# A hybrid flow step on one NeuronCore: weight loads from the Fourier branch on issued by GpSimd in place of SyncE

## The chip, the core and the metric

The kernel runs on one NeuronCore of one Trainium2 chip. In the profile the core's engines are called PE (TensorE, matrix multiplication), PEld (its weight loads), DVE (VectorE), ACT (ScalarE), POOL (GpSimd) and SP (SyncE, which here only issues DMAs). DMAs are issued from three places, SP, ACT and POOL, each with a queue of its own; an engine works off its own instructions, DMA issues among them, in one fixed order, and an instruction that waits for a semaphore keeps everything behind it on the same engine waiting.

The metric is the device time of one execution in microseconds, as the median of several runs.

## What is computed

One layer of a backbone that mixes tokens in three parallel branches, for 2048 sample tokens and 128 prompt tokens of width 1024. Cut to what matters here, the reference is:

```python
proj = jnp.einsum('btd,de->bte', xn, w_in)
qkv, beta, dec, z_a, u_b, v_b, z_b, x_c, z_c, gates = jnp.split(proj, points, axis=-1)
...
o, s_f, s_b = delta_bidir(q, k, v, g, beta, s0_f, s0_b)       # branch A, chunks of 64 in a scan
o_b = chunk_sgu(u_b, v_b, sgu_norm_g, w_spatial, b_spatial) * jax.nn.silu(z_b)   # branch B
o_c = fourier_mix(x_c, grid) * jax.nn.silu(z_c)               # branch C, Fourier over tokens
...
br = jnp.stack([o_a, o_b, o_c], axis=2)
pb = jnp.einsum('btnw,nwd->btnd', br, w_branch)
gt = jax.nn.sigmoid(gates.reshape(B, T, N_BRANCH, D_MODEL))
merged = jnp.einsum('btnd,btnd->btd', gt, pb)
return jnp.einsum('btd,de->bte', merged, w_out), s_f, s_b
```

Everything is float32. The kernel reaches that accuracy with float16 matmuls: each operand is split into a scaled high part and the remainder, and a product takes three matmuls.

## The kernel before, in words

**The long row of matmuls.** The input projection is cut into blocks of 128 output columns: 60 blocks of w_in, 512 KB each, and with the last 24 of them (the merge gates) 24 blocks of w_branch, 256 KB each. They are used in one order, which `wlist` holds: 4 blocks of z_a, 12 of q, k and v, 4 of v_b, 8 of u_b and z_b in turn, then from number 28 on 8 of x_c and z_c in turn (the Fourier branch), and from number 36 on a gate block and a w_branch block in turn, branch B first, then C, then A. A block is multiplied with all 2176 tokens, in five token blocks (four of 512, one of 128), by `gemm_T` at line 250.

**How a block gets ready.** `read_w` (line 291 is its DMA's issue) loads a block into a staging tile of tag `wst`, of which there are two. `converting` then works in four steps: ACT squares the block to sum it (line 315), PE and DVE make a scale of the sum (lines 264 and 277 to 279), ACT writes the scaled high part (line 327), DVE the remainder (line 328). Only after line 328 is the staging tile free for the load after next. `weight_step`, called after each token block, takes one such step; `read_next` issues the next load two steps after a conversion has ended, and at most two blocks ahead. Two other users share the tag `wst`: `gate_rows` (line 1773) and the rows at the very end (lines 1907 and 1920); their loads are issued by SP.

**The second string of work.** Branch A is not done ahead of or after these matmuls but between them. A generator (`delta`) is advanced by `pace` a step at a time as the matmuls go on: first `prep` for the 17 token chunks, with `base_inverse` (POOL and DVE in turn, lines 1114 and 1115), then `scan` (34 steps: the chunks forwards, then backwards). A step of the scan loads from SP its chunk's arrays (ES at line 1171, N at 1175, sn at 1177, sk at 1268, skn at 1270, sv at 1272, sqk at 1322) and does short matmuls; POOL copies ES into T and R (lines 1188 and 1190) and scales skn (line 1295) and kn (line 1298). After the last gate block the products are merged (POOL adds into mrow, line 1739, and stores it) and multiplied with w_out.

**Who decides the order.** The program's text gives priorities. The order on each engine, SP's and POOL's queues included, is laid down when the program is built, by a planner that plays through a time line with a cost for every instruction (`TileContext(nc, schedule_with_timeline_sim=True)`). At run time that order is fixed; only semaphores decide when each instruction goes.

**Queues.** `load` (line 284) issues on SP; early in the program, while `turn_of` is set, it also fixes the order of the loads, and from about the third block on it is a plain `SY.dma_start`. POOL so far issues stores only: qkv, kv, nd, br, the merged rows, tw and pa. `G` is the wrapper around GpSimd; it passes `dma_start` on as it is.

Of the kernel before, what the change touches and what calls it, by code (L numbers as in the profile page):

```python
# [34 lines left out]
CQ = 545  # L35
FS = 4096.0
VS = 2048.0
ADA_D = (6, 7, 12, 13, 14, 15)
TBS = [(0, 512), (512, 512), (1024, 512), (1536, 512), (2048, 128)]

# [80 lines left out]
def _by_block(w, starts, width=P):  # L121


    w = np.asarray(w)
    return np.ascontiguousarray(np.stack([w[:, c0:c0 + width].reshape(-1, P, width).transpose(1, 0, 2).reshape(P, -1) for c0 in starts]))
# [17 lines left out]
def _ada_blocks(w):  # L143


    wide = _by_block(w[:, 0:2 * D], range(0, 2 * D, 2 * P), 2 * P).reshape(8, P, 2, D).transpose(0, 2, 1, 3).reshape(16, P, D)
    return np.ascontiguousarray(np.stack([w[:, b * P:(b + 1) * P].T if b in ADA_D else wide[b] for b in range(16)]))

# [46 lines left out]
def hybrid_flow_kernel(ctx: ExitStack, tc: tile.TileContext, x_prompt, x_sample, state_delta, c, c_ctx, w_ada,  # L195
# [4 lines left out]
    G, V, A, PE = [_InTurn(tc, e_) for e_ in (nc.gpsimd, nc.vector, nc.scalar, nc.tensor)]  # L200
# [9 lines left out]
    def sb(pl, shape, tag, dt=F32, bufs=None):  # L210
        kw = {} if bufs is None else {"bufs": bufs}
        return pl.tile(list(shape), dt, tag=tag, name=nm(tag), **kw)
# [69 lines left out]
    def load_w(src, nkt, cols=P, hi=None, lo=None, tag="w", bufs=5):  # L282
        return convert(read_w(src, nkt, cols, tag), nkt, cols, hi, lo, tag, bufs)
# [3 lines left out]
    def load(dst, src):  # L287


        if turn_of[0] is None:  # L290
            return SY.dma_start(dst, src)
        with tc.issue_after(turn_of[0].ins):
            turn_of[0] = SY.dma_start(dst, src)
        return turn_of[0]

    def read_w(src, nkt, cols=P, tag="w"):
        st = sb(wp, [P, nkt, cols], "wst" if cols == P else tag + "st", bufs=2 if cols == P else 1)
        load(st, src.rearrange("p (k c) -> p k c", c=cols))
        return st

    bsums = sb(cp, [P, 27], "bsums")
# [65 lines left out]
    wdone, wnext, wread, wlate, bwp, wsteps = [], [0], [], [0], [], []  # L367

    def read_next(p_=None):
        if p_ is not None:  # L370
            st = sb(p_, [P, D], "ab", bufs=7).rearrange("p (k c) -> p k c", k=KT)
            load(st, wlist[len(wread)][0].rearrange("p (k c) -> p k c", k=KT))
            wread.append(st)
        elif len(wread) < min(len(wdone) - len(wsteps) + 2, len(wlist)):
            src, nkt, tag, bufs = wlist[len(wread)][0:4]
            wread.append(read_w(src, nkt))
# [275 lines left out]
    load_xt(1)  # L652
    behind = load(cst[:, P:_CF], consts[:, P:_CF])
    bdst = read_w(w_bd, KT, 16, "d")
    turn_of[0] = None
    bound(1)
# [830 lines left out]
    vg = sb(bp, [P, 4], "vg", bufs=1)  # L1487
    V.tensor_scalar(vg, pc[:, 44:48], winv_, 1.0 / VS, ALU.mult, ALU.mult)
    vinv = sb(ep, [P, 4], "vinv", bufs=1)
# [17 lines left out]
    for t in range(NCH):  # L1507
# [12 lines left out]
        made = A.activation(v2[:, 1], vn, AF.Square, accum_out=ss)  # L1520
        V.tensor_scalar(ss, ss, 1.0 / WB / VS ** 2, EPS / VS ** 2, ALU.mult, ALU.add)
        G.tensor_tensor(ss, ss, mhalf, ALU.pow)
# [20 lines left out]
    for g in range(4):  # L1543
# [5 lines left out]
        for ti, (t0, tn) in enumerate(TBS):  # L1549
            st = vrow[:, t0:t0 + tn]  # L1550
# [638 lines left out]
```

## Time and profile before

| | |
|---|---|
| time, median of 3 runs | 2138.12 us (2137.19 to 2139.33) |
| the profiled execution, its time | 2138.49 us |
| its span in the trace | 2136.7 us |
| PE busy | 2081.9 us, 97% of the span |
| DVE, ACT, POOL busy | 62%, 50%, 40% |
| DMA by SP's queue | 290.58 MB, 42.3% of the DMA engines' time |
| DMA by POOL's queue | 65.89 MB, 8.2% |
| DMA by ACT's queue | 44.05 MB, 6.0% |

A page of the profile comes from one execution. "Busy" counts work, not waits, and not the issuing of DMAs. A row of the timeline reads: start, duration, engine and source line, operation, what is written and read, shapes, and in brackets how long the engine had been idle and who ended that. A row of the waits reads: who waited for whom, us in total, how often, the longest. In a row of the windows the engines' busy times are followed by the clock that PE was granted (1.00 is full speed), the share of the DMA engines and GB/s. A row of the issues reads: written and read, the queue, how often, size, median us from issue to landing.

### The profile page before, as it was taken

Reading aid. Unit: us, or ns where it says so; the run is one execution under the profiler, and the core shown is the slowest. Engines: PE = TensorE matmul, PEld = TensorE weight load, DVE = VectorE, ACT = ScalarE, POOL = GpSimd, SP = SyncE. Lnnn points to the kernel's source line nnn. Section 1 sums busy time; section 2 is a strip of 40 time slices with the busy share of each in tenths; the row PEclk is TensorE's granted clock in tenths of the full one; section 3 lists DMA queues with packets and bytes.
Section 4 is the critical chain, followed back from the end, with each engine's and each line's share of the span. In section 5 each row is a group of like instructions: output and inputs, shape, how many; then the busy total and the mean of one; then the engine's idle time right before and its main releaser. Section 6 shows DMA issues by size and latency. Waiting matters only on the chain.

```text
span 2136.7 us, 42553 instructions
## 1 busy us (share of the span) xinstructions
PE 2081.9 (97%) x16133; PEld 1196.5 (56%) x16133; DVE 1326.9 (62%) x2945; ACT 1059.7 (50%) x2456; POOL 844.5 (40%) x1089
## 2 busy tenths in 40 slices
PE   7999999999999999989999999999999999999998
PEld 4454444455555678778565556565655444444443
DVE  6656854379777786556755555866665554666245
ACT  5554744465665664445644445765653443453112
POOL 0321332225465554543321233355542234333464
PEclk9999999999999999999999999999999999999999
DMA  9525722177767744444655555767764644456862
GB/s 354 221 78 188 271 103 103 62 222 232 254 222 247 217 162 133 110 133 128 228 178 168 168 162 185 236 203 233 210 207 131 218 163 165 173 193 236 343 221 89
DMA packets 222286, 403.24 MB, mean 189 GB/s; under 512 B 39225, under 2 KB 109137, under 8 KB 219265
## 3 DMA queue, kind: packets, MB, share of 16 engines
q1 hardware_dynamic: 167040, 290.58, 42.3%
q0 software_dynamic: 15216, 65.89, 8.2%
q10 hardware_dynamic: 39824, 44.05, 6.0%
q8 instruction: 127, 2.08, 0.4%
q14 instruction: 79, 0.64, 0.1%
HBM read 258.19 MB, written 142.24 MB: 187 GB/s over the span
## 4 chain that ended last, share of the span: by engine, by line
PE 53%; DVE 7%; DMA 5%; POOL 4%; ACT 3%; issue 3%; SPq 0%; ACTq 0%; POOLq 0%; DVEq 0%
PE b L250 52%; POOL E L1115 1%; DMA tw<-tw 1%; DVE XB L1114 1%; POOL st L1466 1%; DMA sqk<-qk 1%; DMA ei<-XB 1%; ACT nd L1066 0%; DMA wst<-in_w_blk_dram 0%; DVE XB L1123 0%; PE b L1382 0%; POOL ss L1024 0%; DMA br<-st 0%; DMA skn<-kv 0%; DVE xh L182 0%
## 5 line engine op out<-in xcount | busy, mean ns | idle before, releaser
L250 PE MATMUL b<-xh,whi 128*128 128x512 f16 (+1 forms) x1920 | 651.0, 348 | 1.7 <-DVE sg L1456 1.6
L250 PE MATMUL b<-xl,whi 128*128 128x512 f16 (+1 forms) x1920 | 651.1, 348 | 0.0
L250 PE MATMUL b<-xh,wlo 128*128 128x512 f16 (+1 forms) x1920 | 650.2, 347 | 0.0
L250 PEld LDWEIGHTS <-whi 128*128 128x128 f16 x3856 | 352.5, 98 | 324.8 <-issue 6.1
L250 PEld LDWEIGHTS <-wlo 128*128 128x128 f16 x1928 | 188.8, 98 | 175.8 <-issue 1.8
L250 PE MATMUL b<-big,bhi 128*128 128x512 f16 (+1 forms) x960 | 250.2, 347 | 0.1
L250 PE MATMUL b<-big,blo 128*128 128x512 f16 (+1 forms) x480 | 163.1, 347 | 0.0
L1739 POOL TENSOR_TENSOR mrow<-mrow,sg 128x512 f32<-128x512 f32 (+1 forms) x80 | 95.3, 1193 | 127.7 <-DVE sg L1738 103.4
L953 POOL TENSOR_TENSOR cy<-cy,raw 128x545 f32<-128x545 f32 (+1 forms) x48 | 65.5, 1390 | 182.7 <-ACT raw L952 182.7
L250 PEld LDWEIGHTS <-xh 128*128 128x128 f16 x1496 | 117.0, 98 | 29.0 <-issue 1.5
L250 PEld LDWEIGHTS <-bhi 128*128 128x128 f16 x960 | 87.5, 98 | 76.7 <-issue 0.2
L1115 POOL TENSOR_TENSOR E<-E,XB 128x31 f32<-128x31 f32 (+15 forms) x155 | 94.6, 610 | 85.3 <-DVE XB L1114 68.6
L250 PEld LDWEIGHTS <-xl 128*128 128x128 f16 x1068 | 98.1, 98 | 45.9 <-DMA tw<-tw 2.4
L1729 ACT ACTIVATE sg<-b,winv 128x512 f32<-128x512 f32 (+1 forms) x120 | 74.0, 617 | 93.4 <-PE b L250 92.4
L1188 POOL COPY T<-ES 32x256 f16<-32x256 f16 x68 | 31.9, 470 | 177.0 <-DMA ES<-ei 144.6
L250 PE MATMUL b<-whi,xh 128*128 128x128 f16 x544 | 92.8, 219 | 0.0
L250 PE MATMUL b<-whi,xl 128*128 128x128 f16 x544 | 92.8, 219 | 0.0
L250 PE MATMUL b<-wlo,xh 128*128 128x128 f16 x544 | 92.8, 219 | 0.0
L328 DVE SCALAR_TENSOR_TENSOR wlo<-wst,wsc,whi 128x1024 f16<-128x1024 f32 x52 | 71.0, 1368 | 30.2 <-ACT whi L327 29.0
L1295 POOL TENSOR_TENSOR skn<-skn,ed 128x512 f32<-128x512 f32 x34 | 37.1, 1090 | 112.6 <-DMA skn<-kv 112.6
L1114 DVE TENSOR_TENSOR XB<-XB,E 128x31 f32<-128x31 f32 (+15 forms) x155 | 54.3, 350 | 41.8 <-POOL E L1115 41.2
L315 ACT ACTIVATE wlo<-wst 128x1024 f16<-128x1024 f32 x52 | 54.8, 1055 | 50.5 <-DMA wst<-in_w_blk_dram 47.2
(531 smaller groups left out, 4315.0 us busy)
## 6 DMA issues: line engine op xcount, KB each, us to landing
wst<-in_w_blk_dram SPq DMA_DIRECT2D x58, 512.0 KB, 5.0
pa<-pa POOLq DMA_DIRECT2D x16, 896.0 KB, 4.6
qkv<-cy POOLq DMA_DIRECT2D x12, 1089.0 KB, 5.3
two<-br SPq DMA_DIRECT2D x24, 512.0 KB, 5.9
mrow<-mrg SPq DMA_DIRECT2D x16, 576.0 KB, 5.1
pa<-pa SPq DMA_DIRECT2D x5, 1792.0 KB
dc<-dec SPq DMA_DIRECT2D x17, 512.0 KB, 4.7
kq<-qkv SPq DMA_DIRECT2D x34, 256.0 KB, 4.7
```

Of the source, the lines that this page charges most:

```text
L250: newest[0] = PE.matmul(out, l, r, start=start, stop=stop, skip_group_check=reopened)
L315: w.squared = A.activation(w.lo, st, AF.Square, accum_out=ss)
L328: w.low = V.scalar_tensor_tensor(w.lo, st, s, w.hi, ALU.mult, ALU.subtract)
L953: G.tensor_tensor(y[:, c0:c1], y[:, c0:c1], raw[:, 1 + c0:1 + c1], ALU.mult)
L1114: V.tensor_tensor(t3, X3[:, 0:k, k:k + 1].to_broadcast([P, k, n_]), E3[:, k:k + 1, k:32].to_broadcast([P, k, n_]), ALU.mult)
L1115: G.tensor_tensor(E3[:, 0:k, k:32], E3[:, 0:k, k:32], t3, ALU.subtract)
L1188: G.tensor_copy(T16[rows(a0, b), :, :, b], ES[0:32, :, 2 * a0 + b, :, wT])
L1295: G.tensor_tensor(h3(kn_), h3(kn_), bc(ed[:, d, t, :], P), ALU.mult)
L1466: G.tensor_tensor(o, sg, src, ALU.mult)
L1729: gated_[0] = A.activation(sg, ps, AF.Sigmoid, scale=gw.inv)
L1739: G.tensor_tensor(mr, mr, sg, ALU.add)
```

## The change

From the 28th entry of the list of weight blocks on (the first block of the Fourier branch), `read_w` issues its DMA through GpSimd. Earlier blocks, and the one load outside the list, still go through `load`. Data, tiles, buffers and the calls around it are the same.

```diff
@@ -35,6 +35,7 @@
 CQ = 545
 FS = 4096.0
 VS = 2048.0
+W_SCAN = 28
 ADA_D = (6, 7, 12, 13, 14, 15)
@@ -295,7 +296,7 @@
 
     def read_w(src, nkt, cols=P, tag="w"):
         st = sb(wp, [P, nkt, cols], "wst" if cols == P else tag + "st", bufs=2 if cols == P else 1)
-        load(st, src.rearrange("p (k c) -> p k c", c=cols))
+        (G.dma_start if len(wread) >= W_SCAN else load)(st, src.rearrange("p (k c) -> p k c", c=cols))
         return st
```

`len(wread)` is the number of blocks read so far, so 56 loads change their issuer: 32 of w_in (8 of x_c and z_c, 24 gates) and 24 of w_branch.

## The prediction, made before the changed kernel was run

> **What bounds the kernel now.** I read the page first (busy shares), then the busy times by stretch, then PE's waits and the granted clock, and last the queues that the change touches.
>
> ```profile
> span 2136.7 us, 42553 instructions
> ...
> PE 2081.9 (97%) x16133; PEld 1196.5 (56%) x16133; DVE 1326.9 (62%) x2945; ACT 1059.7 (50%) x2456; POOL 844.5 (40%) x1089
> ```
>
> PE is the bound: 2081.9 of 2136.7 us, so the whole run holds 54.8 us without a matmul. The change removes no matmul; it can only act on that idle time and on the clock that PE is granted. POOL, which gets the new work, is 40% busy. The profiled execution took 2138.49 us, 1.79 us more than its span; the median of the runs shown, 2138.12 us, lies 0.37 us below it, and the sum below is made against 2138.49.
>
> The loads that move begin with weight block 28. Of the 80 loads of line 291 into the staging tile they are the last 56: the first is issued at 654.24 us, the last at 1891.63 us (SP's timeline, first fence; POOL's timeline, second).
>
> ```profile
> 654.24 0.35 SPq L291 DMA_DIRECT2D wst<-in_w_blk_dram  x1
> ...
> 1891.63 0.38 SPq L291 DMA_DIRECT2D wst<-in_w_brb_dram  x1
> ```
> ```profile
> 654.38 1.40 POOL L1024 TENSOR_TENSOR ss<-ss,mhalf 128x4 f32<-128x4 f32 x1 [0.34 <-DVE ss L1023]
> ...
> 1891.73 0.71 POOL L1883 DMA_DIRECT2D pa<-pa  x1 [3.31 <-DVE pa L1826]
> ```
>
> Cut there, and at the borders of the scan's start and of the output stage, the stretches are these (columns: length, busy PE, PEld, DVE, ACT, POOL, then the granted clock):
>
> ```profile
> 0.00:654.00 654.00, 634.67 (x3985) 334.63 (x3986) 432.68 (x829) 363.15 (x769) 220.36 (x292) 0.99 0.57 194
> 654.00:885.00 231.00, 226.11 (x2395) 163.81 (x2394) 168.35 (x400) 130.31 (x362) 129.95 (x197) 0.99 0.52 167
> 885.00:1040.00 155.00, 140.59 (x1906) 112.16 (x1904) 92.49 (x244) 77.27 (x193) 67.79 (x106) 0.96 0.50 148
> 1040.00:1650.00 610.00, 606.39 (x5353) 359.50 (x5352) 375.00 (x953) 324.89 (x849) 220.84 (x292) 1.00 0.62 194
> 1650.00:1925.00 275.00, 275.00 (x1534) 133.98 (x1533) 158.37 (x371) 117.30 (x201) 101.13 (x109) 1.00 0.52 181
> 1925.00:2136.70 211.70, 199.13 (x971) 92.42 (x969) 99.98 (x152) 46.80 (x85) 104.42 (x95) 0.98 0.60 223
> ```
>
> PE's idle time is 19.3 us before the first moved load, then 4.9, 14.4, 3.6 and 0.0 in the four stretches that hold moved loads, and 12.6 after the last of them. Within the change's reach are 22.9 us, most of them in the 155 us around the start of the scan. Three pieces in that reach also run at half clock; the row before the last shows PE idling 2.9 of 6.4 us just ahead of it:
>
> ```profile
> 799.00:805.80 6.80, 6.00 (x52) 5.37 (x50) 6.24 (x24) 2.92 (x9) 3.11 (x7) 0.50 0.39 147
> ...
> 915.00:921.80 6.80, 6.05 (x70) 5.73 (x70) 4.45 (x13) 2.99 (x10) 0.85 (x3) 0.50 0.43 119
> 1028.00:1034.40 6.40, 3.48 (x45) 2.31 (x43) 3.79 (x11) 3.64 (x9) 6.29 (x10) 1.00 0.73 242
> 1034.40:1041.20 6.80, 5.40 (x42) 4.04 (x43) 5.72 (x16) 6.80 (x17) 0.23 (x1) 0.50 0.65 221
> ```
>
> A piece of 6.8 us at 0.50 costs at most 3.4 us, the three 10.2. No rearrangement of these loads can therefore gain more than 22.9 + 10.2 = 33.1 us. What the stalls in reach wait for:
>
> ```profile
> PE b L250 <- DMA ES<-ei: 4.1, 2, 2.3
> ...
> PE b L250 <- DVE Q L1219: 1.5, 1, 1.5
> PE b L250 <- DMA N<-n: 1.4, 1, 1.4
> ```
>
> None names a converted weight; the DMA waits, 4.1 + 1.4 = 5.5 us, are for the scan's own loads from SP's queue.
>
> **What is removed.** From SP, 56 issues, 32 of the first kind and all 24 of the second (durations are minimum/median/maximum in ns):
>
> ```profile
> L291 SPq DMA_DIRECT2D wst<-in_w_blk_dram x56: 328/345/1032, 76.4 to 1884.4; - x56
> L291 SPq DMA_DIRECT2D wst<-in_w_brb_dram x24: 327/346/1025, 906.0 to 1891.6; - x24
> ```
>
> 56 x 0.346 = 19.4 us of SP's time, and the waits that SP stands in before them, between 654 and 1925 us mostly for the vector engine to finish with a staging buffer:
>
> ```profile
> SPq L291 <- DVE wlo L328: 40.7, 14, 14.1
> ...
> SPq L291 <- DVE blo L328: 25.4, 13, 5.4
> ```
>
> That is 66.1 us in 27 waits, nearly all with nothing else due on SP. What SP gets back matters where the next load of the scan follows at once. At the scan's start one load lies in such a place (SP, then POOL, which waits for what SP issues next):
>
> ```profile
> 905.95 0.36 SPq L291 DMA_DIRECT2D wst<-in_w_brb_dram  x1
> 906.59 0.34 SPq L1270 DMA_DIRECT2D skn<-kv  x1
> ```
> ```profile
> 909.37 1.04 POOL L1295 TENSOR_TENSOR skn<-skn,ed 128x512 f32<-128x512 f32 x1 [2.81 <-DMA skn<-kv]
> ```
>
> Taking it away lets the loads behind it go 0.4 us earlier, at the place where PE waits for ES and N. I book 0.4 us of gain there and nothing elsewhere: over the 610 us of 1040 to 1650, where most of the moved loads lie, PE idles 3.6 us in all, so a scan load that comes sooner has nothing to shorten.
>
> **What is added.** To POOL, 56 issues. POOL issues loads of neither kind today; the nearest row is its store of the same 512 KB, and its time to landing stands beside SP's weight load:
>
> ```profile
> L1045 POOL DMA_DIRECT2D kv<-tok x17: 546/600/640, 451.7 to 798.4; - x17
> ```
> ```profile
> wst<-in_w_blk_dram SPq DMA_DIRECT2D x58, 512.0 KB, 5.0
> ...
> kv<-tok POOLq DMA_DIRECT2D x17, 512.0 KB, 5.1
> ```
>
> So 56 x 0.600 = 33.6 us of POOL's time (bounds 56 x 0.546 and 56 x 0.640: 30.6 and 35.8), 1.6% of the span, and landings alike within 0.1 us. To see who is pushed I laid the 56 issue times into POOL's timeline, first and last as quoted above: the load starts when POOL is free, lasts 0.60 us, and pushes the next operation by what overlaps. 18 of the 56 push something, by 0.66 us at most and 7.9 us in sum; the other 38 fall into idle time. The load itself waits 9.4 us in sum for POOL's operation in flight, 0.17 us each; with the 0.1 us of the landing it comes 0.27 us later than from SP. The cover is POOL's own 60% of idle time; without it the whole 33.6 us would be serial. Between the matrix engine and a pushed operation lies the slack of the scan and of the merge, which on the evidence of 3.6 and 0.0 us of idle time swallows 0.66 us; bounds for what reaches PE are 0 and 7.9 us, and I take 0.
>
> **The added wait.** In POOL's queue a load stands until the vector engine has released its buffer; behind it wait the scan's copies into T and R, the scaling of skn and kn, the merge's additions to mrow and the stores of the merged rows. Those feed ACT, DVE and then PE. One cycle of the scan (DVE, SP, ACT, POOL, PE in turn):
>
> ```profile
> 1213.89 1.28 DVE L328 SCALAR_TENSOR_TENSOR wlo<-wst,wsc,whi 128x1024 f16<-128x1024 f32 x1 [0.35 <-ACT whi L327]
> ```
> ```profile
> 1215.21 0.35 SPq L291 DMA_DIRECT2D wst<-in_w_blk_dram  x1
> ```
> ```profile
> 1219.41 1.06 ACT L315 ACTIVATE wlo<-wst 128x1024 f16<-128x1024 f32 x1 [1.89 <-DMA wst<-in_w_blk_dram]
> ```
> ```profile
> 1215.46 0.82 POOL L1188 COPY T<-ES 32x256 f16<-32x256 f16 x2 [9.00 <-DMA ES<-ei]
> ```
> ```profile
> 1222.97 0.77 PE L250 MATMUL b<-S,sk 128*128 128x128 f16 x11 [0.36 <-DVE S L1232]
> ```
>
> The load goes 0.04 us after the vector engine lets go of the buffer: DVE is the releaser, not SP's queue, so POOL cannot send it sooner. It lands 4.2 us later with ACT already waiting. ACT is held 1.89 us; behind it the scan's S is late and PE loses 0.36. Over the reach ACT loses
>
> ```profile
> ACT wlo L315 <- DMA wst<-in_w_blk_dram: 21.2, 13, 3.1
> ```
>
> 21.2 us in 13 waits. A load later by 0.27 us adds 13 x 0.27 = 3.5 us to ACT; at PE, in the ratio of the cycle shown (0.36 to 1.89), 0.7 us. Bounds: 0, and 3.5 if all of it shows.
>
> **The sum** against 2138.49: minus 0.4 (SP), plus 0 (POOL's issues), plus 0.7 (ACT), less the same 0.7, which I allow for the scan loads that now go earlier elsewhere: 2138.1, which against the median is 2137.7. By the bounds alone the change lies between -5.5 (both DMA waits gone) and 7.9 + 3.5 = +11.4.
>
> The Trainium skill, "SBUF — State Buffer" (sections "SBUF: two separate sides" and "Who interferes with whom"), speaks against the change: GpSimd writes the descriptors of its own DMAs through a port that VectorE locks while it runs a copy, a cast or a tensor_scalar in a two-port mode, so that such a DMA looks blocked, and SP's or ACT's queue is advised. By that rule the sum would be rival 3's. The trace so far does not bear it out: kv<-tok lands within 0.1 us of SP's load.
>
> **The rivals.**
> 1. *SP's queue was the brake at the scan's start.* For it: the waits for ES and N. Against it: a single weight load is issued there. If all of it goes, with the half-clock piece at 915 behind it: 5.5 + 3.4 = 8.9 us, 2129.6.
> 2. *POOL is held* (the slower side). The 66.1 us that SP stood waiting are stood by POOL, 2.45 us at a time, and a third of them (18 of 56 loads have work close behind) stops an operation of the scan: 9 x 2.45 = 22 us, half of it covered by other matmuls, 11 us: 2149.5. It decides once a hold exceeds the slack that PE's fixed order leaves. Against it: where DVE itself waits for POOL (the E chain of the base inverse), a load cannot stand ahead of the operation that its own releaser needs, and POOL mostly idles when the buffer comes free.
> 3. *POOL's issue is held while DVE runs a copy.* For it the trace has nothing, as the landings above show. The longest DVE copy in the reach is
>
> ```profile
> L1107 DVE COPY XB<-XB 64x1024 f32<-64x1024 f32 x3 | 3.2, 1064 | 3.9 <-DMA XB<-nd 3.8
> ```
>
> so a load held for all of one is 1.06 us later; 13 loads with ACT waiting lose 13.8 us of ACT, 2.6 us of PE by the ratio above: 2141.1, still inside what I call the same.
> 4. *The order is laid anew.* The program's order on every engine is planned when it is built, with a cost for each instruction; a DMA that costs another engine time shifts that plan from 654 us on. One cluster of stalls like that of 1028 to 1041.2 us comes or goes: by the two rows above 2.9 + 1.4 = 4.3 us of idle time and 3.4 of half clock, 7.7 us, so 2130.8 or 2146.2.
> 5. *It doesn't do what it says*: block numbers counted otherwise, nothing moved, 2138.5.
>
> **How the numbers follow.** About 0.2%, 4.3 us, is what a measurement here can tell from no change. Forecast: 0.37, its own range 2133.8 to 2142.4; inside that range lie rival 3 (0.02) and rival 5 (0.01) too. Rival 1: 0.16. Rival 2: 0.15. Rival 4: 0.15 faster, 0.14 slower. So faster 0.31, same 0.40, slower 0.29. Both signs together hold more than the middle, and the order laid anew may add to either; for 8 in 10 the range goes from 2126 (rival 1 and part of 4) to 2150 (just past rival 2).
>
> **What would show it.** The issue table should list wst from POOL 56 times and from SP 26, with 0.6 us an issue and landings near 5 us. PE's busy time should stay at 2082 and its idle time between 654 and 1925 near 23 us; POOL's line should grow by about 34. Rival 1 shows as shorter waits for ES and N, rival 2 as POOL waiting at line 291 for DVE and PE idle behind T, R or kn, rival 4 as half-clock pieces at other places. An idle time in the reach under 15 or over 32 us would prove me wrong, as would a change before 654 us.

## The result, and the profile after

The changed kernel took 2149.12 us (median of ten runs, 2144.42 to 2151.80), the kernel before 2140.44 us beside it (ten runs, 2137.19 to 2146.32): a ratio of 1.0034, 95% interval 1.0022 to 1.0047. (Here and below the ratio is taken over all runs of both kernels; it is not the quotient of the two medians, which would be 1.0041 here.) It is slower by 8.7 us by the medians and by 7.3 us by the means, where 0.4 us less was forecast. The profiled execution took 2149.3 us.

The page of the changed kernel, span and busy times:

```profile
span 2147.5 us, 42591 instructions
...
PE 2084.4 (97%) x16133; PEld 1198.0 (56%) x16133; DVE 1331.0 (62%) x2945; ACT 1060.4 (49%) x2456; POOL 877.4 (41%) x1145
```

The matmuls are the same 16133. Of the 10.8 us that the span grew, PE's idle time makes 8.3 (63.1 against 54.8) and its busy time 2.5. POOL is busy 32.9 us longer. The issues of the moved line (minimum/median/maximum in ns) and the time to landing:

```profile
L299 POOL DMA_DIRECT2D wst<-in_w_blk_dram x32: 532/577/641, 652.6 to 1893.4; - x32
L299 POOL DMA_DIRECT2D wst<-in_w_brb_dram x24: 541/587/647, 911.8 to 1897.5; - x24
```
```profile
wst<-in_w_blk_dram POOLq DMA_DIRECT2D x32, 512.0 KB, 4.6
wst<-in_w_blk_dram SPq DMA_DIRECT2D x26, 512.0 KB, 5.7
```

56 issues, near 0.6 us each, none over 0.65, the 512 KB landing in 4.6 us: the change does what it says at the price that was forecast. The busy times by stretch, in the columns used before:

```profile
0.00:654.00 654.00, 634.58 (x3994) 334.85 (x3994) 432.99 (x832) 364.89 (x775) 222.72 (x294) 1.00 0.57 194
654.00:885.00 231.00, 219.62 (x2298) 157.93 (x2297) 167.68 (x393) 126.29 (x351) 133.29 (x204) 0.99 0.54 168
885.00:1040.00 155.00, 143.23 (x1979) 115.89 (x1976) 95.00 (x242) 77.92 (x194) 67.65 (x109) 0.96 0.46 138
1040.00:1650.00 610.00, 602.84 (x5308) 357.73 (x5309) 372.63 (x946) 322.60 (x834) 235.90 (x319) 0.99 0.62 193
1650.00:1925.00 275.00, 275.00 (x1526) 133.97 (x1525) 156.45 (x365) 117.58 (x211) 108.87 (x122) 1.00 0.53 181
1925.00:2147.50 222.50, 209.12 (x1037) 97.68 (x1035) 106.28 (x170) 51.12 (x94) 108.97 (x100) 0.98 0.58 218
```

Length less PE's busy time gives its idle time: 19.4 us ahead of the first moved load (19.3 before), then 11.4 (4.9), 11.8 (14.4), 7.2 (3.6), 0 (0), and 13.4 (12.6) behind the last. The loss sits in two stretches, 654 to 885 with 6.5 us and 1040 to 1650 with 3.6. What PE waited for in the first of them, after and then before (who waited for whom, us in total, times, longest):

```profile
PE b L251 <- DVE yT L1643: 3.3, 1, 3.3
PE b L251 <- DVE xc L1573: 2.8, 2, 1.7
```
```profile
PE b L1049 <- DVE tok L1033: 1.1, 1, 1.1
```

Before, no wait in that stretch is longer than 1.1 us. The new one of 3.3 us, seen in the timelines of DVE and PE:

```profile
872.14 0.69 DVE L1124 SCALAR_TENSOR_TENSOR XB<-E,XB 128x512 f16<-128x512 f32 x1 [1.03 <-ACT XB L1123]
873.14 2.56 DVE L1124 SCALAR_TENSOR_TENSOR XB<-E,XB 128x512 f16<-128x512 f32 x3 [0.31 <-ACT XB L1123]
875.62 0.58 DVE L1642 TENSOR_TENSOR yT<-b,us 128x256 f32<-128x256 f32 x1
876.05 0.59 DVE L1643 TENSOR_TENSOR yT<-b,us 128x256 f32<-128x256 f32 x1
```
```profile
876.70 0.23 PE L251 MATMUL b<-whi,xh 128*128 128x128 f16 x1 [3.33 <-DVE yT L1643]
```

On DVE the four copies that end the base inverse stand ahead of the two yT operations that PE needs. In DVE's timeline of before (line numbers one lower) the two stand the other way round:

```profile
870.73 0.60 DVE L1641 TENSOR_TENSOR yT<-b,us 128x256 f32<-128x256 f32 x1
871.18 0.60 DVE L1642 TENSOR_TENSOR yT<-b,us 128x256 f32<-128x256 f32 x1
...
881.24 0.69 DVE L1123 SCALAR_TENSOR_TENSOR XB<-E,XB 128x512 f16<-128x512 f32 x1 [1.55 <-ACT XB L1122]
```

No operation of this scene is slower, and none waits for POOL's load; their order is another one. A second scene lies at the end of the scan (changed kernel: SP, DVE, PE):

```profile
1561.78 4.42 SPq L1176 DMA_DIRECT2D N<-n  x6
1566.43 0.40 SPq L1774 DMA_DIRECT2D wst<-in_w_ada_dram  x1
```
```profile
1570.05 0.62 DVE L475 TENSOR_SCALAR sg<-wst,scT 128x256 f32<-128x256 f32 x2 [2.77 <-DMA wst<-in_w_ada_dram]
...
1576.67 0.68 DVE L1233 SCALAR_TENSOR_TENSOR u<-sv,u 128x512 f16<-128x512 f32 x1
```
```profile
1577.40 0.77 PE L251 MATMUL b<-u,kn 128*128 128x128 f16 x11 [2.21 <-DVE u L1233]
```

SP issues the load for `gate_rows` right behind six loads of N; DVE has `gate_rows`' operations (lines 475 and 477) ahead of the scan's u, stands 2.77 us for that load, and PE 2.21 us for u. Before, the same load was issued 1.8 us earlier, DVE stood 0.85 us for it (SP, then DVE), and no u kept PE waiting:

```profile
1564.60 0.40 SPq L1773 DMA_DIRECT2D wst<-in_w_ada_dram  x1
```
```profile
1568.19 0.65 DVE L474 TENSOR_SCALAR sg<-wst,scT 128x256 f32<-128x256 f32 x2 [0.85 <-DMA wst<-in_w_ada_dram]
```

This scene is less clean than the first. Before, too, six loads of N went ahead of that load, and `gate_rows`' operations stood ahead of a u; and of the six issues one now takes 1.81 us (1.58 in the repeat of the same kernel), where the longest took 0.50 before. Why it does is not shown. Behind such waits lie pieces at half clock (the 0.50 in the third column from the end) at places where before has none:

```profile
895.80:899.20 3.40, 3.40 (x39) 3.40 (x40) 1.11 (x2) 1.87 (x4) 2.75 (x5) 0.50 0.52 116
1578.50:1581.90 3.40, 3.40 (x10) 1.20 (x9) 1.41 (x6) 2.13 (x6) 1.42 (x3) 0.50 0.81 303
```

They do not explain the loss: the mean granted clock is 0.991 in both executions, and in the repeat of the changed kernel the same two windows have a clock of 1.00.

So the order was laid anew. Set side by side instruction by instruction, the orders of the two programs differ on the matrix engine in 6731 lines (its order has 31311), all of them between the first moved load and the end of the scan. The orders of DVE, ACT, POOL and SP differ too.

### The profile page after: what moved, and what is told of

The parts are those of the page before. It is cut to its first block, busy times and chain, and to the rows that moved or that the text cites. A ratio compares the mean times of both kernels' runs of the same rounds, so it can differ in the third digit from the quotient of the medians.

```text
span 2147.5 us, 42591 instructions
## 1 busy us (share of the span) xinstructions
PE 2084.4 (97%) x16133; PEld 1198.0 (56%) x16133; DVE 1331.0 (62%) x2945; ACT 1060.4 (49%) x2456; POOL 877.4 (41%) x1145
## 5 line engine op out<-in xcount | busy, mean ns | idle before, releaser
L328 ACT ACTIVATE whi<-wst,wsc 128x1024 f16<-128x1024 f32 x52 | 59.4, 1143 | 41.5 <-DVE wsc L279 41.4
```

What stands on the lines that cost most here:

```text
L328: w.made = A.activation(w.hi, st, AF.Copy, scale=s)
```

## The experiments

**Theory A**: the planner's new order costs the time, and the moved loads themselves nearly nothing. **Theory B**: POOL's issues, and POOL standing at line 299 for a buffer, cost it as they run; then it grows with the number of loads. **Theory C**, taken up later: it is the loads' leaving SP, by whatever engine.

The way to tell them apart came from comparing orders. A single load issued by POOL can change the matrix engine's order in thousands of lines (block 56: 3702, block 58: 3182, block 61: 2340), while 42 loads moved together can leave it as it was. So kernels can be made that move many loads with the old order nearly kept, and others that move one load and get a new order. The number of lines depends on what is compared of an instruction and on how far a displaced one shifts the rest; what counts is whether it is none, hundreds or thousands.

| loads issued otherwise | lines of PE's order that differ | PE idle, 654 to 1925 us, in the profile | ratio to before (95%) |
|---|---|---|---|
| none (before) | 0 | 22.9 | 1 |
| 56, POOL (the change; the result above) | 6731 | 30.3 | 1.0034 (1.0022 to 1.0047) |
| 56, POOL (again) | 6731 | 29.8 | 1.0042 (1.0026 to 1.0058) |
| 48, POOL (from the first gate block) | 4872 | 28.2 | 1.0035 (1.0022 to 1.0049) |
| 14, POOL | 3880 | 23.0 | 1.0004 (0.9991 to 1.0018) |
| 4, POOL (31, 39, 56, 58) | 3497 | 26.7 | 1.0014 (1.0004 to 1.0025) |
| 1, POOL (56) | 3702 | 25.9 | 1.0040 (1.0025 to 1.0056) |
| 1, POOL (58) | 3182 | 31.5 | 1.0058 (1.0041 to 1.0075) |
| 1, POOL (58), again | 3182 | 31.4 | 1.0059 (1.0041 to 1.0078) |
| 1, POOL (61) | 2340 | 25.9 | 1.0015 (1.0000 to 1.0029) |
| 42, POOL | 0 | 24.6 | 1.0013 (1.0002 to 1.0023) |
| 52, POOL | 592 | 22.0 | 1.0001 (0.9992 to 1.0010) |
| 52, POOL and 4, ACT | 650 | 23.5 | 0.9999 (0.9988 to 1.0010) |
| 56, ACT | 666 | 23.1 | 1.0007 (0.9995 to 1.0018) |
| 1, ACT (58) | 0 | 25.0 | 1.0003 (0.9991 to 1.0015) |
| none, POOL busy 40 us longer, ahead of 49 us | 0 | 21.7 | 1.0001 (0.9992 to 1.0009) |

The idle time is 1271.0 us less PE's busy time between 654 and 1925 us, of one execution each; the ratio is that of many runs. Everything with the order nearly kept idles 21.7 to 25.0 us, however many loads were moved. The kernels with thousands of changed lines idle 23.0 to 31.5. The two ranges overlap, and so do the ratios (the kernels with 14 loads, with four and with block 61 lost little or nothing): a new order can cost time and need not.

The edits below are written against the kernel before and cut to the lines that matter: `load(st, ...)` stands for the whole call, and constants and the declaration of a tile are left out.

**The whole change, again**, with no edit.

> The change as it is, all 56 loads from POOL, measured again beside the kernel before on one chip. Both theories were made from its first result (ratio 1.0034, about 7.3 us), so both expect 1.002 to 1.005 again; under 1.001 would say that there is no slowdown to explain.

2145.85 us, ratio 1.0042, with PE idle in the same two stretches (11.5 and 7.4 us). The loss comes again.

**42 loads, those that leave the matrix engine's order as it was.**

```diff
+RELAY = (28, 30, 31, 35, 36, 39, 40, 46, 52, 56, 58, 60, 61, 63)
-        load(st, ...)
+        (G.dma_start if len(wread) >= W_SCAN and len(wread) not in RELAY else load)(st, ...)
```

> 42 of the 56 loads from POOL, chosen so that the order of PE's instructions is that of the kernel before, row for row, and those of DVE and ACT differ in few places; 14 loads stay on SP. Theory A (the new order of the engines, which the planner lays down, costs the time, not the issuing from POOL): ratio 0.999 to 1.001, PE idle between 654 and 1925 us near 23 us as before. Theory B (issues and waits in POOL's queue cost the time as they run): 42/56 of 7.3 us, 5.5 us, ratio 1.0026, idle time near 29 us or more, ended by POOL's copies, kn or mrow.

2140.43 us, ratio 1.0013 (1.0002 to 1.0023): for three quarters of the loads about a third of the loss, by the interval at most a little over half. Theory B in proportion would have 1.0026 by the expectation, 1.0032 by the repeat above. Theory A missed too, by a little: it allowed 1.001.

**The other 14 alone**, the numbers listed above.

```diff
-        load(st, ...)
+        (G.dma_start if len(wread) in RELAY else load)(st, ...)
```

> The other 14 loads alone from POOL; PE's order then differs from the kernel before in several thousand rows. Theory A: most of the whole change's loss, or another number as the stalls happen to fall, 1.001 to 1.005, and at least three half-clock pieces at places where the kernel before has none. Theory B: 14/56 of 7.3 us, 1.8 us, ratio 1.0009.

2140.78 us, 1.0004. The loss of the 56 is not the sum of the 42 and the 14 (1.0013 and 1.0004 against 1.0042): neither half holds it. Theory A's number (1.001 to 1.005) was missed, and B's 1.0009 lies in the interval. That the loss does not add up is no surprise to A, since the 14 alone get another order than the 56; but it had no way to say that this order would be a harmless one.

**Block 56 alone.**

```diff
-        load(st, ...)
+        (G.dma_start if len(wread) == 56 else load)(st, ...)
```

> One single load from POOL, that of block 56 (a gate block of branch C); POOL gets 0.6 us of work more, but PE's order from there on differs in several thousand rows. Theory A: anything from minus 4 to plus 6 us (0.998 to 1.003), with stalls that stand elsewhere than before after about 1350 us. Theory B: 0.1 us, ratio 1.0000.

2146.62 us, 1.0040: a single load, issued at 1387.3 us, costs as much as all of them. That ends theory B in proportion to the loads as the main cause. Theory A had it up to 1.003 only: it foretells that a new order can cost, not how much.

**All 56 from ScalarE.**

```diff
+        (A.dma_start if len(wread) >= W_SCAN else load)(st, ...)
```

> All 56 loads leave SP's queue, but are issued by ScalarE in place of GpSimd. The planner's order then stays nearly as before (666 of 31311 lines of the matrix engine's order differ, against 6731 for the whole change; none of GpSimd's own work changes). Before on the same chip is taken as 2138.9. Theory A (the order laid anew costs the time): within 0.15% of before, 2135.7 to 2142.1. Theory B (GpSimd's issues and waits cost it as they run): nothing of it is left, so the same 2138.9 or less. A third theory, C (the loss comes from the loads leaving SP, by whatever engine they go: they collide with the scan's own loads): 1.003 to 1.005, 2145.3 to 2149.6. So this run holds A and B against C.

2140.35 us, 1.0007, not to be told from before. Theory C falls: the loads may leave SP.

**POOL busy, loads left on SP.**

```diff
+        if len(wread) >= W_SCAN:
+            for _ in range(2):
+                G.memset(blank, 0.0)
         load(st, ...)
```

> The loads stay on SP; in their place GpSimd gets, at each of the 56 blocks, two memsets of 128x288 float32 that wait for nothing, about 0.6 us together, so that it is busy some 34 us longer, as with the change. The order of the matrix engine's instructions is that of before, line for line. Theory A: 1.000, at most 1.0015 (2138.9 to 2142.1). Theory B in its form 'GpSimd's 0.6 us an issue push its other work': 1.002 or more, 2143.2 and up.

2138.75 us, 1.0001. POOL's busy time rose by 40.4 us (844.5 to 884.9), but not where the loads are. The memsets wait for nothing, and the planner put all 112 at the program's start (the trace's row; the last two figures are the first and the last start):

```profile
L303 POOL MEMSET blank<- x112: 327/338/342, 0.9 to 48.1; 128x288 f32 x112
```

The last one starts some 600 us ahead of the first weight load in question. So this run doesn't do what its expectation says, and tells nothing about POOL's work beside the scan; for that there are only the runs in which POOL issues loads.

**Block 61 alone.**

```diff
-        load(st, ...)
+        (G.dma_start if len(wread) == 61 else load)(st, ...)
```

> One load alone, that of block 61, is issued by GpSimd; the planner's order then differs from before in 2340 lines of the matrix engine, from about 1640 us on. Theory A: a new order can come out either way, so a time that differs from that of block 56 alone (1.0040): between 0.998 and 1.005, 2134.6 to 2149.6, and where it is slower, stalls of the matrix engine at places where before has none. Theory B: one issue of 0.6 us is 1/56 of the cost, 1.0001, 2139.1.

2141.54 us, 1.0015 with an interval from 1.0000: inside theory A's wide range and no test of theory B by itself. The load is issued at 1493.6 us; the expectation's 1640 us is too late.

**From the first gate block on, 48 loads.**

```diff
-        load(st, ...)
+        (G.dma_start if len(wread) >= W_SCAN + 8 else load)(st, ...)
```

> The 48 loads from the first gate block on are issued by GpSimd, the 8 of the Fourier branch by SP as before; the matrix engine's order differs from before in 4872 lines, all after about 885 us. Theory A: the 6.5 us that the whole change loses between 654 and 885 us are not there, the stalls after 1040 us may be: 1.000 to 1.003, 2138.9 to 2145.3. Theory B (in proportion to the number of loads): 48/56 of 0.42%, 1.0036, 2146.6.

2147.26 us, 1.0035. This went against theory A's range (up to 1.003) and met theory B's number. The part of A that held: PE idles 6.5 us between 654 and 885 us, not 11.4. But 28.2 us in all from 654 to 1925. The next run had to decide.

**52 loads, all but 31, 39, 56 and 58.** With only these four left on SP the planner comes back to nearly the old order.

```diff
+RELAY = (31, 39, 56, 58)
-        load(st, ...)
+        (G.dma_start if len(wread) >= W_SCAN and len(wread) not in RELAY else load)(st, ...)
```

> 52 of the 56 loads are issued by GpSimd, all but those of blocks 31, 39, 56 and 58, which stay on SP; with these four left out the planner comes back to nearly the order of before (592 lines of the matrix engine differ, against 6731 for all 56). Before is taken as 2139.5. Theory A (the order laid anew costs the time): like the 42 loads, 1.000 to 1.0015, 2139.5 to 2142.7. Theory B (GpSimd's issues and waits cost it as they run, in proportion to the loads): 52/56 of 0.42%, 1.0039, 2147.8. With the 48 loads from the first gate block on at 1.0035, this run decides between the two.

2139.22 us, 1.0001. More loads than in the run before it, and the loss is gone. POOL works and waits as with the whole change (page, and POOL's waits):

```profile
PE 2082.5 (97%) x16133; PEld 1196.1 (56%) x16133; DVE 1328.9 (62%) x2945; ACT 1059.0 (50%) x2456; POOL 873.1 (41%) x1141
```
```profile
POOL wst L300 <- DVE wlo L330: 40.1, 11, 9.6
POOL wst L300 <- DVE blo L330: 26.0, 13, 7.8
```

It stands 66.1 us for these two alone, up to 9.6 us at a time, and the kernel is as fast as before. The windows of the two stretches that lost time in the changed kernel show 5.5 and 1.6 us of idle PE, against 11.4 and 7.2 there:

```profile
654.00:885.00 231.00, 225.54 (x2379) 162.80 (x2378) 169.65 (x398) 130.80 (x363) 132.87 (x204) 0.99 0.52 167
...
1040.00:1650.00 610.00, 608.38 (x5361) 360.56 (x5361) 375.99 (x954) 326.59 (x855) 237.06 (x318) 1.00 0.61 195
```

**Those four alone.**

```diff
-        load(st, ...)
+        (G.dma_start if len(wread) in (31, 39, 56, 58) else load)(st, ...)
```

> Only the four loads that the run with 52 leaves out (31, 39, 56, 58) are issued by GpSimd; 3497 lines of the matrix engine's order differ from before. Theory A: a new order from the Fourier branch on, so anything between 0.999 and 1.005, likeliest 1.002 to 1.004 (2143.8 to 2148.1), above the run with 52 loads. Theory B: 4/56 of 0.42%, 1.0003, 2140.1.

2141.48 us, 1.0014 with an interval from 1.0004: above the run with 52, below A's likeliest range, above B's 1.0003. Four loads from POOL cost more than 52, but less than the 56.

**Block 58 alone.**

```diff
-        load(st, ...)
+        (G.dma_start if len(wread) == 58 else load)(st, ...)
```

> One load alone, that of block 58, from GpSimd; 3182 lines of the matrix engine's order differ, from about 1580 us on. Theory A: another draw from the orders that the planner can come to, 0.998 to 1.005 (2135.2 to 2150.2); if it is near 1.000, a new order is not dear by itself, only some are. Theory B: 1.0001, 2139.7.

2151.03 us, 1.0058, beyond the top of A's range: one load costs more than all. The expectation puts the place of the load some 150 us too late: it is at 1430.86 us on SP before (below), and the new order starts near it.

**All 56 off SP, the four from ScalarE, the 52 from GpSimd.**

```diff
+        (load if len(wread) < W_SCAN else A.dma_start if len(wread) in RELAY else G.dma_start)(st, ...)
```

> All 56 loads leave SP: 52 go to GpSimd, and those of blocks 31, 39, 56 and 58 to ScalarE; 650 lines of the matrix engine's order differ from before. It is the whole change with the old order nearly kept. Theory A: 1.000 to 1.0015, 2139.5 to 2142.7. Theory B: 1.0039, 2147.8. Theory C (the loss comes from the loads leaving SP): 1.004, 2148.

2139.09 us, 0.9999. This is the whole change but for four issuers, with the old order nearly kept, and it takes the time of before. B and C both asked for 1.004.

**Block 58 alone, again.** The first profile of this kernel had lost several microseconds against before ahead of the moved load, where the orders are the same.

> The load of block 58 alone from GpSimd once more, the same kernel as in the run that gave 1.0058. Before is taken as 2139.1. Its first profile lost about half of its 10 us against before ahead of block 58, where both kernels have the same order. If that half was chance, the time comes out at 1.002 to 1.005 (2143.4 to 2149.8) and the profile runs level with before up to about 1520 us, within 3 us; the loss after 1520 us, 5 to 7 us, comes again. If the early half comes again as well, the new order after 1520 us is not all of the cause, and theory A lacks something.

2150.24 us, 1.0059, above the range that was named (the 1520 us of the expectation is a miscount as well). To see where the time goes, take a step that both kernels do in the same place, the remainder of a weight block: in DVE's timeline of before, and then of this kernel, one just ahead of the moved load and one behind the scan:

```profile
1428.53 2.30 DVE L328 SCALAR_TENSOR_TENSOR wlo<-wst,wsc,whi 128x1024 f16<-128x1024 f32 x1 [0.96 <-ACT whi L327]
...
1474.39 1.12 DVE L1345 SCALAR_TENSOR_TENSOR S<-S,egl,b 128x128 f32<-128x128 f32 x4
1475.43 0.84 DVE L259 TENSOR_SCALAR oss<-oss 128x4 f32<-128x4 f32 x1
...
1679.52 1.28 DVE L328 SCALAR_TENSOR_TENSOR wlo<-wst,wsc,whi 128x1024 f16<-128x1024 f32 x1 [0.96 <-ACT whi L327]
```
```profile
1429.55 1.44 DVE L329 SCALAR_TENSOR_TENSOR wlo<-wst,wsc,whi 128x1024 f16<-128x1024 f32 x1 [0.96 <-ACT whi L328]
...
1474.38 0.27 DVE L260 TENSOR_SCALAR oss<-oss 128x4 f32<-128x4 f32 x1 [5.16 <-ACT of L1376]
...
1475.21 1.11 DVE L1346 SCALAR_TENSOR_TENSOR S<-S,egl,b 128x128 f32<-128x128 f32 x4
...
1689.41 1.28 DVE L329 SCALAR_TENSOR_TENSOR wlo<-wst,wsc,whi 128x1024 f16<-128x1024 f32 x1 [0.96 <-ACT whi L328]
```

It is 1.0 us late at the first and 9.9 us at the second: 8.9 us are lost behind the moved load, none to speak of ahead of it, so the early loss of the first profile was that execution's. The load itself, on SP before and on POOL here:

```profile
1430.86 0.33 SPq L291 DMA_DIRECT2D wst<-in_w_blk_dram  x1
```
```profile
1433.18 0.58 POOL L299 DMA_DIRECT2D wst<-in_w_blk_dram  x1
```

And what PE waited for from 1430 us to that second mark, here and then before:

```profile
PE b L1383 <- ACT o L1379: 3.2, 2, 2.4
PE b L251 <- DVE S L1233: 2.6, 2, 1.7
PE b L251 <- DVE Q L1220: 0.8, 1, 0.8
```
```profile
PE b L1382 <- ACT o L1378: 0.6, 1, 0.6
PE b L250 <- ACT Q L1186: 0.2, 1, 0.2
```

With four smaller ones the waits of this kernel make 8.1 us, against 0.8 before; none of them is for a weight. At 1474 us DVE has stood 5.16 us at line 260 (oss, for the norm of the scan's output), with the S that PE needs next behind it in DVE's order; PE loses 0.84 us by it. Before, S goes ahead of oss (lines 1345 and 259 above). The load came 2.3 us later than from SP; the first stall of PE is 23 us further on (0.8 us at 1456), the last 205 (2.4 us at 1638).

**Block 58 alone, from ScalarE.**

```diff
-        load(st, ...)
+        (A.dma_start if len(wread) == 58 else load)(st, ...)
```

> The load of block 58 alone leaves SP for ScalarE; the orders of the matrix and the vector engine stay as before, line for line (6 lines differ on ScalarE). Theory A: 1.000, within 0.1% (2137.0 to 2141.2). If it were the load's leaving SP at this place, and not the order, that costs the time: 1.004 to 1.006, 2147.7 to 2151.9.

2139.28 us, 1.0003. The same load, off SP at the same place, with the orders of PE and DVE kept line for line, costs nothing that can be told.

**What follows.** Theory A is shown as far as such runs can: with the order nearly kept, 52 issues by POOL, their 66 us of standing and 56 loads off SP cost between -0.12% and +0.10% together; with a new order a single load costs 0.58% and, again, 0.59%. It is shown as a cause, not as a measure: the kernels with 14 loads, with block 56, with 48 loads and with block 58 all came out beyond the range that it had given. The run with 42 loads (1.0013, interval above 1) is the one that could hold a small cost of POOL's own; the runs with 52 don't confirm it.

One rival comes from how the kernels were chosen: all that keep the order leave blocks 31, 39, 56 and 58 off POOL, so a cost of POOL's issuing just these would fit them as well. The kernel with 14 loads and that with four speak against it: both issue all four from POOL, and take 1.0004 (0.9991 to 1.0018) and 1.0014 (1.0004 to 1.0025), less than block 56 or block 58 alone (1.0040 and 1.0058).

What stays open is which of the moved instructions decide: taking away one stall (yT behind XB, u behind `gate_rows`) without touching the rest wasn't tried, as an edit there can lay the order anew as well. Nor do the runs show what in the planner's own time line made it choose so. No version beats before.

## Why the prediction was wrong

**The step that failed** is not a term of the sum but what the sum was laid on: "I laid the 56 issue times into POOL's timeline", that is, of before, and what was pushed there was weighed against "the slack that PE's fixed order leaves". That timeline does not survive the change. The sum has no term for a new order, which puts it at nothing. The new order was rival 4, with 0.14 on its slower side, and the forecast of no change, which needs the old order, had 0.37. The runs turn that round: with all 56 loads off SP and the order nearly kept, the time is that of before (0.9999), as the sum has it; with the new order it is 1.0034 and 1.0042 of it. The wide range, 2126 to 2150, held 2149.12 by luck: its upper end was set by rival 2, which is not what happened.

Point by point:

- *The bound.* PE stayed the bound with the same matmuls; its idle time went from 54.8 to 63.1 us. Right. The idle time within reach went from 22.9 to 30.3 us, still under the 32 that I had set as proof against me: the limit was too wide, since 7 us there is most of the loss.
- *Nothing before 654 us.* Right: 19.3 and 19.4 us idle.
- *SP's relief, -0.4 us.* Too small to see. Moving all 56 to ScalarE left 1.0007. The waits for ES and N (4.1 and 1.4 us before) did not vanish: they are 1.3 and 2.6 us in the changed kernel, 5.2 and 1.1 with the 52 and the 4.
- *POOL's issues, 33.6 us, 0 reaching PE.* Right in size: POOL's busy time rose by 32.9 us. That nothing reaches PE is borne out by the run with 52 loads, where POOL is busy 28.6 us longer at 1.0001; the run with the memsets is no proof, as they ran elsewhere.
- *ACT held longer, +0.7 us.* Not seen: with the new order ACT waits 19.8 us in 12 waits for the blocks (21.2 in 13 before).
- *Rival 1, SP the brake.* Refuted: no kernel that frees SP is faster.
- *Rival 2, POOL held.* POOL does stand at the moved line for DVE, and up to 9.6 us in the run with 52, four times the mean of my estimate. It costs nothing that can be told there: 66.1 us of it at 1.0001.
- *Rival 3, POOL's issue held while DVE runs a copy.* Not seen, and hardly tested: no issue of the 56 took more than 0.647 us, and the 512 KB loads land in 4.6 us; but DVE's copies, casts and tensor_scalars fill only some 62 of the 1271 us between 654 and 1925, and a single issue (0.53 us at 1832.3) overlaps one of them, for 0.22 us. So what the Trainium skill, "SBUF — State Buffer", section "SBUF: two separate sides", says of DMAs from GpSimd while VectorE runs a copy in a two-port mode is neither borne out nor contradicted by the loads of this kernel.
- *Rival 4, the order laid anew.* This is what happened, on the slower side, and nearly at its price: 7.7 us forecast, 8.7 and 7.0 us measured (2149.12 against 2140.44, 2145.85 against 2138.86). The form was other: not one cluster of 4.3 us of waits and 3.4 of half clock, but waits of 1 to 3.3 us at several places. That the size came out so near is luck: by the medians the other new orders cost between 1.9 and 11.9 us. The sign that I named for it, half-clock pieces at other places, showed, but it is a poor one: such pieces stand elsewhere in the repeat of the same kernel too.

The chance of rival 4 was set from a single sentence, that a DMA which costs another engine time shifts the plan from 654 us on. The traces of before could not say which way; but nothing in them said either that the plan would stay, and the forecast was worked out as if it would.

## What to carry to other kernels

Where a planner lays down the order on every engine, the issuer of a DMA is one of its inputs, and an edit of it has two prices: what it costs as it runs, and what the new order costs. Here the first was zero within 0.12% for the kernel with all 56 loads off SP, and the second lay between nothing and 0.59%, with no relation to the number of loads moved. To tell them apart, compare the orders of the two programs first, then run the largest part of the edit that keeps the old order beside the smallest part that changes it; a time change that comes with a changed order says nothing yet about the engine or the queue that the edit was meant for.

## What the runs showed beside this

- POOL issued the 512 KB loads in 0.53 to 0.64 us; ScalarE needed 0.33 to 0.37 us for the four loads that it issues in the mixed kernel, SP 0.35 in the median.
- Executions of one and the same kernel spread widely: before ran between 2133.76 and 2146.99 us, 0.6%, over all the times on record, taken on several chips, so that the three runs shown first (2137.19 to 2139.33) had looked far tighter than such times are, and a profile of one execution can be several microseconds off its kernel's median in either direction (block 56: 2143.04 profiled, 2146.62 the median; the memsets: 2141.25 and 2138.75).
- The granted clock falls to 0.50 in pieces of 3.4 us or 6.8 and 10.2 us, in the scan of the changed kernel behind waits of PE of 1.2 to 2.6 us, while its longest wait, 3.33 us at 876.7, has none behind it. Each 3.4 us of such a piece can cost up to 1.7 us beside the wait itself. They stand at other places from one execution of a kernel to the next.
